# Two engines for the memory banks, a direct split of the sample queries, and a finer first cut of the input

## The chip, the cores and the metric

The kernel runs on one core of a Trainium2 chip. The core has a matrix engine (TensorE, PE in the profile), VectorE (DVE), ScalarE (ACT), GpSimd (POOL) and SyncE (SP), which here only issues transfers. Each engine works through its own list of instructions in a fixed order and waits on semaphores for the others. The metric is the device time of one execution in microseconds; three runs of the kernel before took 2074.03, 2075.16 and 2075.26 us.

## The reference

One layer of a hybrid decoder step: 256 prompt tokens and 8 x 8 sample tokens, 320 rows in all, width 2048, all in fp32. What matters here is the beginning of the layer, the keys and values of the memory, and the queries:

```
def memory_kv(mem, p):
    m = rms_norm(mem, p['norm_mem'])
    k = (m @ p['w_k']).reshape(b_, N_MEM, XA_HEADS, XA_HEAD_DIM)
    v = (m @ p['w_v']).reshape(b_, N_MEM, XA_HEADS, XA_HEAD_DIM)
...
    h = rms_norm(x, p['norm_mix_pre'])
    proj = h @ p['w_in']
...                      # convolution, RWKV-7 mix, w_out, residual
    h = rms_norm(x, p['norm_xa_pre'])
    q = (h @ p['w_q']).reshape(b_, t_, XA_HEADS, XA_HEAD_DIM)
    s = jnp.einsum('bthd,bmhd->bhtm', q, mem_k) * (XA_HEAD_DIM ** -0.5)
...                      # softmax, values, w_o, then a gated ConvFFN
```

The prompt attends to 256 memory tokens whose keys and values are computed here and are outputs too; each of the 8 sample requests has its own keys and values in a cache.

## The kernel before

All products are made of f16 halves: an fp32 number times a power of two is rounded to f16 (the high part, on ScalarE), and what is left over is the low part (on VectorE, one scalar_tensor_tensor). A product then takes three matmuls: high x high, high x low and low x high. `split` (L191 to L193) does this for activations. `wpiece` (L145 to L157) does it for weights: a transfer into `raw` on SP's queue, `whi` on ScalarE (L154), `wlo` on VectorE (L155), in a ring of three buffers each. A piece is 128 x 1024 numbers, so every piece costs VectorE and ScalarE one long operation, and PE uses it right behind.

The start, `rows_in` (L196 to L221): x lies in three tiles of rows (128, 128 and 64), loaded in four groups of 512 columns, three transfers a group. PE turns each 128-column block (L207, through `turn`, L61) into a bank `psn` (five of them), ScalarE writes the high part of h (L213), VectorE the low part (L214). `take(q)` then lets out steps of the first dense product (192 columns of w_in), 8 after each of the first three groups. ScalarE also squares the rows for the norm (L218), with `late` putting a square behind PE's last instruction so far.

The memory projections, `mem_steps` (L940 to L956): w_k has four blocks of 512 columns, w_v four. For each block, two banks `accs[0]` and `accs[1]` (128 memory tokens each) take 3 x 16 matmuls; at the end both are scaled into an SBUF tile (called `memo` in the trace, as it is a part of that tile) and sent off. The program text has both scalings on ScalarE:

```
            for j in range(2):
                kv = kvst[j]
                A.activation(kv, accs[j], AF.Copy, scale=mst[:, j, 7:8])
                SP.dma_start(dst[0, 0, j * P:(j + 1) * P, n, :], kv)
```

The first six blocks (four of w_k, two of w_v; in the text below blocks 0 to 5) run in the pool `psA`, in which these banks are only two, so that a block's first product waits until the block before has left. The last two (blocks 6 and 7) run in `psB`, whose banks are four.

The queries, `q_evac` (L1222 to L1234): for each of 16 feature blocks VectorE scales the bank into `qf` (L1226); the prompt's 256 columns are split into `qp` (ScalarE L192, VectorE L193); then ScalarE scales the 64 sample columns in place (L1228), and GpSimd casts them into `qs` (L1231) and subtracts to get their low part (L1232). `qf` has two buffers. The sample scores `pss` are products with `qs`.

The order: an instruction of ScalarE, VectorE, GpSimd and SP gets its place by a scheduler that simulates times and takes the ready instruction of the highest priority; `tc.high_priority(offset=...)` moves what is inside ahead by so many places (AHEAD is 1200). PE's order in the first part is written by hand, in a planner that lets several generators take turns by a modelled clock. So a change of one engine's operation can move others.

Of the kernel before, what the change touches and what calls it, by code (L numbers as in the profile page):

```python
# [12 lines left out]
AF = mybir.ActivationFunctionType  # L13
ALU = mybir.AluOpType
AX = mybir.AxisListType
PSUM = bass.MemoryType.PSUM

P = 128
# [12 lines left out]
SX = 32.0  # L31
# [4 lines left out]
AHEAD = 1200  # L36
# [10 lines left out]
def hybrid_step_kernel(ctx: ExitStack, tc: tile.TileContext, I, O):  # L47
# [148 lines left out]
    def rows_in(pool, psum, loads, gcol, op, ssq, take):  # L196
        tl = []
        for j, (src, rows) in enumerate(loads):
            tl.append((pool.tile([P, D], F32, name=f"xt{j}"), rows))
        for q in range(4):  # L200
            qc = slice(q * 512, (q + 1) * 512)
            with tc.high_priority(offset=(2 * AHEAD if q == 0 else AHEAD)):
                for (xt, rows), (src, _) in zip(tl, loads):
                    SP.dma_start(xt[:rows, qc], src[:, qc])
            with tc.high_priority(offset=600):
                for f in range(4 * q, 4 * q + 4):
                    ps = psum.tile([P, 512], F32, tag="m", bufs=5, name="psn")  # L207
                    c = 0
                    for xt, rows in tl:
                        turn(ps[:, c:c + rows], xt[:rows, f * P:(f + 1) * P], ident[:rows, :rows])  # L210
                        c += rows
                    oh, ol = op(f)
                    A.activation(oh[:, :c], ps[:, :c], AF.Copy, scale=gcol[:, f:f + 1])  # L213
                    V.scalar_tensor_tensor(ol[:, :c], ps[:, :c], gcol[:, f:f + 1], oh[:, :c], ALU.mult, ALU.subtract)  # L214
            take(q)
            for j, (xt, rows) in enumerate(tl):
                jk = pool.tile([P, 512], F16, tag="njk", bufs=2, name="njk")
                sq = A.activation(jk[:rows], xt[:rows, qc], AF.Square, accum_out=ssq[:rows, j, q:q + 1])  # L218
                if q in (0, 1, 2, 3):
                    late(sq)  # L220

    w_in = I["w_in"][0]
    psA = tc.alloc_tile_pool(name="psA", bufs=3, space=PSUM)
# [10 lines left out]
    with tc.tile_pool(name="p0", bufs=1, side="right", reuse_waits="tile") as p0:  # L234

        def vpt(name="vpt"):
            return psA.tile([P, 512], F32, tag="x", bufs=1, name=name)

        with tc.high_priority(offset=3 * AHEAD):
            ld0 = vr.tile([16, P], F32, tag="ld0", bufs=1, name="ld0")  # L240
            SP.dma_start(ld0, I["norm_mix_pre"][0].rearrange("(t p) -> t p", p=P))
        pt = vpt()
        turn(pt[:, :16], ld0, ident[:16, :16])
        V.tensor_scalar(gx[:, 0:16], pt[:, :16], SX, None, ALU.mult)
        lora_evac = {}
        first_ = dense_steps(psA, w_in, KD, [(5120, 192)], [(0, 0, 96), (0, 96, 96)], opn(h1), T, lambda mi, acc: lora_evac["small"](mi, acc))
        xp, xs_ = I["x_prompt"][0], I["x_sample"].rearrange("b t d -> (b t) d")
        rows_in(p0, psA, [(xp[0:128], 128), (xp[128:256], 128), (xs_, 64)], gx[:, 0:16], opn(h1), xss, lambda q: [next(first_) for _ in range((8, 8, 8, 0)[q])])
        ldm = vr.tile([26, P], F32, name="ldm")
        SP.dma_start(ldm[0:24, :], I["rwkv_mu"][0, 0:3072].rearrange("(t p) -> t p", p=P))  # L250
        SP.dma_start(ldm[24:26, :], I["rwkv_mu"][0, 3264:3520].rearrange("(t p) -> t p", p=P))
        ld3 = vr.tile([2, 96], F32, name="ldL")
        SP.dma_start(ld3, I["rwkv_mu"][0, 3072:3264].rearrange("(t p) -> t p", p=96))
        ld5 = vr.tile([NB, 3520], F32, name="ldS")
        SP.dma_start(ld5, I["state_shift"][0])
        ld2 = vr.tile([80, P], F32, name="ldR")
        for n, nm in enumerate(vR_names):
            SP.dma_start(ld2[8 * n:8 * n + 8, :], I[nm][0].rearrange("(t p) -> t p", p=P))
        ld4 = vr.tile([CW, W], F32, name="ldC")
        SP.dma_start(ld4, I["conv_dw"][0])  # L260
        ld = vr.tile([112, P], F32, name="ldD")
        for n, nm in enumerate(vD_names):
            SP.dma_start(ld[16 * n:16 * n + 16, :], I[nm][0].rearrange("(t p) -> t p", p=P))
        pt = vpt()
        turn(pt[:, :26], ldm, ident[:26, :26])
        turn(pt[:96, 128:130], ld3, ident[:2, :2])
        V.tensor_copy(vecR[:, 80:106], pt[:, :26])
        V.tensor_copy(muL, pt[:96, 128:130])
        pt = vpt()
        for t in range(26):  # L270
            c0 = t * P + (192 if t >= 24 else 0)
            turn(pt[:, NB * t:NB * t + NB], ld5[:, c0:c0 + P], ident[:NB, :NB])
        for z in range(2):
            turn(pt[:96, 256 + NB * z:256 + NB * z + NB], ld5[:, 3072 + 96 * z:3168 + 96 * z], ident[:NB, :NB])
        V.tensor_copy(stR.rearrange("p b t -> p t b"), pt[:, 0:208].rearrange("p (t b) -> p t b", b=NB))
        V.tensor_copy(stL.rearrange("p b t -> p t b"), pt[:96, 256:272].rearrange("p (t b) -> p t b", b=NB))
        pt = vpt()
        turn(pt[:, :80], ld2, ident[:80, :80])
        V.tensor_copy(vecR[:, 0:80], pt[:, :80])
        pt = vpt()  # L280
        for c in range(8):
            turn(pt[:, 32 * c:32 * c + CW], ld4[:, c * P:(c + 1) * P], ident[:CW, :CW])
        V.tensor_copy(cdw, pt[:, 0:256].rearrange("p (c j) -> p c j", j=32)[:, :, 0:CW])
        pt = vpt()
        turn(pt[:, :112], ld, ident[:112, :112])
        V.tensor_copy(vecD, pt[:, :112])
        with tc.high_priority(offset=0):
            xm = p0.tile([P, 3, 2], F32, name="xm")
            V.tensor_reduce(xm[:, :, 0], xss[:, :, 0:4], AX.X, ALU.add)
            V.tensor_scalar(xm[:, :, 0], xm[:, :, 0], 1.0 / D, 1e-6, ALU.mult, ALU.add)  # L290
            G.tensor_tensor(xm[:, :, 1], xm[:, :, 0], nhalf[:, 0:3], ALU.pow)
            V.tensor_scalar(xm[:, :, 1], xm[:, :, 1], 0.5 * INV, None, ALU.mult)
            dg = p0.tile([P, 3, P], F32, name="xdg")
            V.tensor_tensor(dg, ident.unsqueeze(1).broadcast_to([P, 3, P]), xm[:, :, 1:2].broadcast_to([P, 3, P]), ALU.mult)
            pt = vpt()
            for j in range(3):
                mm(pt[:, j * P:j * P + (P if j < 2 else 64)], ones, dg[:, j, 0:P if j < 2 else 64], True, True)
            V.tensor_copy(rh, pt[:, :T])
# [641 lines left out]
    def mem_steps(src, dst, ns, psum):  # L940
        for n in ns:
            accs = [psum.tile([P, 512], F32, tag="acc", name="acck", **({"bufs": 2} if psum is psA else {})) for _ in range(2)]
            for k0 in range(0, KD, 2):
                hi, lo = wpiece(src, k0, 2, [(n * 512, 512)])
                for j in range(2):
                    for k in range(2):
                        kt, c, cols = k0 + k, slice(k * 512, (k + 1) * 512), slice(j * P, (j + 1) * P)
                        mo = memo[kt // 8][:, kt % 8]
                        mm(accs[j], mo[:, 0, cols], hi[:, c], kt == 0, False)
                        mm(accs[j], mo[:, 1, cols], hi[:, c], False, False)  # L950
                        mm(accs[j], mo[:, 0, cols], lo[:, c], False, kt == KD - 1)
                        yield 1.5
            for j in range(2):
                kv = kvst[j]
                A.activation(kv, accs[j], AF.Copy, scale=mst[:, j, 7:8])  # L955
                SP.dma_start(dst[0, 0, j * P:(j + 1) * P, n, :], kv)  # L956


# [263 lines left out]
    def q_evac(f0):  # L1222
        def f_(mi, acc):
            f = f0 + mi
            qf = bw.tile([P, T], F32, tag="qf", name="qf")
            V.tensor_tensor(qf, acc[:, :T], rq, ALU.mult)  # L1226
            split(qp[:, f, 0, :], qp[:, f, 1, :], qf[:, 0:256], SX)
            A.activation(qf[:, 256:320], qf[:, 256:320], AF.Copy, scale=SX)  # L1228
            v_ = qf[:, 256:320].rearrange("p (j b e) -> p j b e", b=2, e=8)
            dh, dl = (qs[f // 4 % 2][:, f % 4, z].rearrange("p j (b e) -> p j b e", e=40)[:, :, :, 0:8] for z in range(2))  # L1230
            G.tensor_copy(dh, v_)  # L1231
            G.tensor_tensor(dl, v_, dh, ALU.subtract)  # L1232
            qdone[0] += 1
        return f_  # L1234

# [429 lines left out]
```

## Time and profile before

| | before |
|---|---|
| median of 3 runs | 2075.16 us (2074.03 to 2075.26) |
| profiled execution | 2076.79 us |
| its span | 2075.1 us |
| PE busy | 2001.3 us, 96% |
| VectorE busy | 1394.6 us, 67% |
| ScalarE busy | 990.9 us, 48% |
| GpSimd busy | 592.1 us, 29% |

The span is the stretch that the profiler sees of one execution; the execution's own time is 1.7 us longer. Busy shares are means over stages that differ. A wait is read from a timeline: an instruction's start, its length, and in brackets how long its engine stood idle before it and what released it. Operations on one engine can overlap a little at their ends, so a start can lie just before the end of the one ahead.

### The profile page before, as it was taken

What the parts mean: (1) busy time and instruction counts of PE and PEld (TensorE: products, weight loads), DVE (VectorE), ACT (ScalarE), POOL (GpSimd) and SP (SyncE); (2) the same over time, 40 slices, a digit from 0 to 9 for tenths busy, and PEclk for the clock granted to TensorE, in tenths of its full rate; (3) what the DMA queues carried; (4) which work ended last, traced back from release to release, by engine and by line L of the source; (5) the groups of instructions that cost most, each with busy time, mean ns of one, the idle gap of its engine ahead of it and who ended that gap; (6) DMA issues with size and microseconds to landing.
All of it is one profiled execution on the core that took longest, in us unless ns stands there. A gap on an engine that the chain in (4) does not pass through costs nothing.

```text
span 2075.1 us, 44953 instructions
## 1 busy us (share of the span) xinstructions
PE 2001.3 (96%) x17941; PEld 1392.5 (67%) x17941; DVE 1394.6 (67%) x2479; ACT 990.9 (48%) x1710; POOL 592.1 (29%) x908
## 2 busy tenths in 40 slices
PE   8989999999999999989999999999999999999998
PEld 6766666666454676556677667777777777777777
DVE  5699787987866636877774696666666666444343
ACT  5444435445545535665663454444444444533331
POOL 3635435444012211300001242444444443000000
PEclk9999999999999999999999999999999999999999
DMA  6543333332547765767765455555555555555552
GB/s 189 149 117 110 88 105 91 107 96 77 174 136 218 235 198 188 242 211 246 251 207 164 131 148 159 162 163 163 163 163 163 163 163 160 162 172 183 163 155 90
DMA packets 301999, 333.34 MB, mean 161 GB/s; under 512 B 33882, under 2 KB 227237, under 8 KB 301764
## 3 DMA queue, kind: packets, MB, share of 16 engines
q1 hardware_dynamic: 301788, 330.46, 53.0%
q8 instruction: 141, 2.31, 0.5%
q14 instruction: 70, 0.57, 0.1%
HBM read 319.90 MB, written 11.22 MB: 160 GB/s over the span
## 4 chain that ended last, share of the span: by engine, by line
PE 79%; DVE 9%; DMA 5%; ACT 2%; issue 2%; POOL 2%; SPq 0%; DVEq 0%; POOLq 0%; ACTq 0%
PE acc L57 62%; PE acck L57 7%; DMA rawkv<-in_cache_mem_v_dram 3%; DVE wlo L155 2%; PE pX L57 1%; DVE cvmix L825 1%; DVE vl L1280 1%; PE pk L61 1%; DMA rawkv<-out_dram 1%; ACT vh L1279 1%; PE psZ L57 1%; PE psX L57 1%; PE pSc L57 1%; PE pU L57 1%; PE pSn L57 0%
## 5 line engine op out<-in xcount | busy, mean ns | idle before, releaser
L57 PE MATMUL acc<-h,whi 128*128 128x320 f16 (+1 forms) x4736 | 984.0, 302 | 11.7 <-DVE h L1163 4.3
L155 DVE SCALAR_TENSOR_TENSOR wlo<-raw,whi 128x1024 f16<-128x1024 f32 (+1 forms) x512 | 626.4, 1226 | 449.6 <-ACT whi L154 446.5
L57 PEld LDWEIGHTS <-whi 128*128 128x128 f16 (+1 forms) x7080 | 686.3, 99 | 279.1 <-issue 13.9
L154 ACT ACTIVATE whi<-raw 128x1024 f16<-128x1024 f32 (+1 forms) x512 | 533.0, 1043 | 596.5 <-PE acc L57 498.8
L57 PE MATMUL acc<-h,wlo 128*128 128x320 f16 (+1 forms) x2368 | 704.1, 302 | 0.0
L57 PEld LDWEIGHTS <-wlo 128*128 128x128 f16 (+1 forms) x3540 | 348.6, 98 | 144.0 <-issue 7.6
L57 PE MATMUL acc<-act,whi 128*128 128x320 f16 x1320 | 269.6, 299 | 0.0
L57 PE MATMUL acc<-act,wlo 128*128 128x320 f16 x660 | 196.6, 299 | 0.0
L57 PE MATMUL acck<-whi,memo 128*128 128x512 f16 x512 | 151.3, 380 | 2.0 <-ACT memo L955 2.0
L825 DVE SCALAR_TENSOR_TENSOR cvmix<-GX,cdw,cvmix 128x320 f32<-128x320 f32 x240 | 144.5, 602 | 1.7
L1510 POOL COPY nF<-U 128x9 f32<-128x9 f32 x88 | 49.3, 560 | 302.0 <-DVE U L1509 299.0
L57 PEld LDWEIGHTS <-memo 128*128 128x128 f16 x768 | 72.7, 98 | 82.4 <-issue 3.5
L1507 POOL COPY U<-stF 128x16 f32<-128x16 f32 x88 | 127.4, 1453 | 0.9 <-ACT stF L1495 0.9
L1145 POOL TENSOR_TENSOR sums<-sums,bsq 128x320 f32<-128x320 f32 x33 | 37.8, 1146 | 241.3 <-ACT bsq L1139 239.7
L57 PE MATMUL acck<-wlo,memo 128*128 128x512 f16 x256 | 95.6, 379 | 0.3 <-DVE wlo L155 0.3
L1515 DVE SCALAR_TENSOR_TENSOR C<-U,fdw,C 128x336 f32<-128x336 f32 x176 | 91.2, 558 | 0.0
L1513 ACT ACTIVATE C<-U,fdw 128x336 f32<-128x336 f32 x88 | 55.8, 659 | 31.3 <-DVE U L1509 30.9
L1508 DVE TENSOR_TENSOR U<-acc,rs 128x256 f32<-128x256 f32 x88 | 36.8, 418 | 39.4 <-PE acc L57 39.4
L1280 DVE SCALAR_TENSOR_TENSOR vl<-rawkv,vh 128x1024 f16<-128x1024 f32 x31 | 37.3, 1224 | 32.4 <-ACT vh L1279 32.2
L1231 POOL CAST qs<-qf 128x64 f16<-128x64 f32 x16 | 10.0, 623 | 161.6 <-ACT qf L1228 161.6
L335 POOL TENSOR_TENSOR pb<-pb,rh 128x256 f32<-128x256 f32 (+1 forms) x28 | 27.4, 980 | 100.3 <-ACT pb L332 86.8
L57 PE MATMUL acc<-oopb,whi 128*128 128x320 f16 x256 | 53.7, 299 | 1.2 <-DVE oopb L193 1.0
(466 smaller groups left out, 2535.7 us busy)
## 6 DMA issues: line engine op xcount, KB each, us to landing
raw<-in_w_up_dram SPq DMA_DIRECT2D x352, 256.0 KB
raw<-in_w_down_dram SPq DMA_DIRECT2D x71, 512.0 KB
raw<-in_w_in_dram SPq DMA_DIRECT2D x52, 512.0 KB
raw<-in_w_in_dram SPq DMA_DIRECT2D x64, 256.0 KB
raw<-in_w_k_dram SPq DMA_DIRECT2D x32, 512.0 KB
raw<-in_w_v_dram SPq DMA_DIRECT2D x32, 512.0 KB
raw<-in_w_out_dram SPq DMA_DIRECT2D x32, 512.0 KB
rawkv<-in_cache_mem_k_dram SPq DMA_DIRECT2D x32, 512.0 KB
```

The costliest lines, as they stand in the source:

```text
L57: pe[0] = TE.matmul(out, lhsT=lhsT, rhs=rhs, start=start, stop=stop, skip_group_check=skip)
L154: A.activation(hi[:, :n], raw[:, :n], AF.Copy, scale=SW)
L155: V.scalar_tensor_tensor(lo[:, :n], raw[:, :n], SW, hi[:, :n], ALU.mult, ALU.subtract)
L335: G.tensor_tensor(pb[:w, 1:257], pb[:w, 1:257], rh[:w, 0:256], ALU.mult)
L825: late(V.scalar_tensor_tensor(o_, i_, cdw[:, c, j:j + 1], o_, ALU.mult, ALU.add))
L1145: (V if f > 11 else G).tensor_tensor(ssum, ssum, sq, ALU.add)
L1280: V.scalar_tensor_tensor(vl, raw, SX, vh, ALU.mult, ALU.subtract)
L1507: G.tensor_copy(us[:, :, 0:2], stF[:, :, :, j])
L1508: V.tensor_tensor(U[:, 2:258], acc[:, 0:256], rf[:, 0:256], ALU.mult)
L1510: G.tensor_copy(nF[:, :, 0, j], U[:, 256:338:10])
L1513: A.activation(c, U[:, 0:336], AF.Identity, bias=fdw[:, 3, j:j + 1], scale=fdw[:, 0, j:j + 1])
L1515: V.scalar_tensor_tensor(c, U[:, t_:t_ + 336], fdw[:, t_, j:j + 1], c, ALU.mult, ALU.add)
```

## The change

Three edits. The first 512 columns of the input are loaded in two groups of 256 columns (six transfers, all at the higher priority), the dense steps are handed out as 2, 6, 8 and 8, and there are 15 squares in place of 12. Of a memory block's two banks the first is scaled on VectorE and the second on ScalarE, both with a priority of 3600 places. The sample part of `qf` is split directly, on ScalarE and VectorE, ahead of the prompt's part; the scaling in place and GpSimd's two operations are gone.

```
@@ -197,13 +197,14 @@
         tl = []
         for j, (src, rows) in enumerate(loads):
             tl.append((pool.tile([P, D], F32, name=f"xt{j}"), rows))
-        for q in range(4):
-            qc = slice(q * 512, (q + 1) * 512)
-            with tc.high_priority(offset=(2 * AHEAD if q == 0 else AHEAD)):
+        cuts = (0, 2, 4, 8, 12, 16)
+        for q, (fa, fb) in enumerate(zip(cuts, cuts[1:])):
+            qc = slice(fa * P, fb * P)
+            with tc.high_priority(offset=(2 * AHEAD if q < 2 else AHEAD)):
                 for (xt, rows), (src, _) in zip(tl, loads):
                     SP.dma_start(xt[:rows, qc], src[:, qc])
             with tc.high_priority(offset=600):
-                for f in range(4 * q, 4 * q + 4):
+                for f in range(fa, fb):
                     ps = psum.tile([P, 512], F32, tag="m", bufs=5, name="psn")
                     c = 0
                     for xt, rows in tl:
@@ -215,9 +216,7 @@
             take(q)
             for j, (xt, rows) in enumerate(tl):
                 jk = pool.tile([P, 512], F16, tag="njk", bufs=2, name="njk")
-                sq = A.activation(jk[:rows], xt[:rows, qc], AF.Square, accum_out=ssq[:rows, j, q:q + 1])
-                if q in (0, 1, 2, 3):
-                    late(sq)
+                late(A.activation(jk[:rows, 0:(fb - fa) * P], xt[:rows, qc], AF.Square, accum_out=ssq[:rows, j, q:q + 1]))
 
     w_in = I["w_in"][0]
     psA = tc.alloc_tile_pool(name="psA", bufs=3, space=PSUM)
@@ -245,7 +244,7 @@
         lora_evac = {}
         first_ = dense_steps(psA, w_in, KD, [(5120, 192)], [(0, 0, 96), (0, 96, 96)], opn(h1), T, lambda mi, acc: lora_evac["small"](mi, acc))
         xp, xs_ = I["x_prompt"][0], I["x_sample"].rearrange("b t d -> (b t) d")
-        rows_in(p0, psA, [(xp[0:128], 128), (xp[128:256], 128), (xs_, 64)], gx[:, 0:16], opn(h1), xss, lambda q: [next(first_) for _ in range((8, 8, 8, 0)[q])])
+        rows_in(p0, psA, [(xp[0:128], 128), (xp[128:256], 128), (xs_, 64)], gx[:, 0:16], opn(h1), xss, lambda q: [next(first_) for _ in range((2, 6, 8, 8, 0)[q])])
         ldm = vr.tile([26, P], F32, name="ldm")
         SP.dma_start(ldm[0:24, :], I["rwkv_mu"][0, 0:3072].rearrange("(t p) -> t p", p=P))
         SP.dma_start(ldm[24:26, :], I["rwkv_mu"][0, 3264:3520].rearrange("(t p) -> t p", p=P))
@@ -286,7 +285,7 @@
         V.tensor_copy(vecD, pt[:, :112])
         with tc.high_priority(offset=0):
             xm = p0.tile([P, 3, 2], F32, name="xm")
-            V.tensor_reduce(xm[:, :, 0], xss[:, :, 0:4], AX.X, ALU.add)
+            V.tensor_reduce(xm[:, :, 0], xss[:, :, 0:5], AX.X, ALU.add)
             V.tensor_scalar(xm[:, :, 0], xm[:, :, 0], 1.0 / D, 1e-6, ALU.mult, ALU.add)
             G.tensor_tensor(xm[:, :, 1], xm[:, :, 0], nhalf[:, 0:3], ALU.pow)
             V.tensor_scalar(xm[:, :, 1], xm[:, :, 1], 0.5 * INV, None, ALU.mult)
@@ -952,7 +951,11 @@
                         yield 1.5
             for j in range(2):
                 kv = kvst[j]
-                A.activation(kv, accs[j], AF.Copy, scale=mst[:, j, 7:8])
+                with tc.high_priority(offset=3 * AHEAD):
+                    if j:
+                        A.activation(kv, accs[j], AF.Copy, scale=mst[:, j, 7:8])
+                    else:
+                        V.tensor_scalar(kv, accs[j], mst[:, j, 7:8], None, ALU.mult)
                 SP.dma_start(dst[0, 0, j * P:(j + 1) * P, n, :], kv)
 
 
@@ -1224,12 +1227,10 @@
             f = f0 + mi
             qf = bw.tile([P, T], F32, tag="qf", name="qf")
             V.tensor_tensor(qf, acc[:, :T], rq, ALU.mult)
-            split(qp[:, f, 0, :], qp[:, f, 1, :], qf[:, 0:256], SX)
-            A.activation(qf[:, 256:320], qf[:, 256:320], AF.Copy, scale=SX)
             v_ = qf[:, 256:320].rearrange("p (j b e) -> p j b e", b=2, e=8)
             dh, dl = (qs[f // 4 % 2][:, f % 4, z].rearrange("p j (b e) -> p j b e", e=40)[:, :, :, 0:8] for z in range(2))
-            G.tensor_copy(dh, v_)
-            G.tensor_tensor(dl, v_, dh, ALU.subtract)
+            split(dh, dl, v_, SX)
+            split(qp[:, f, 0, :], qp[:, f, 1, :], qf[:, 0:256], SX)
             qdone[0] += 1
         return f_
```

Counted over the whole program, VectorE gets 8 scalings of 128x512 and 16 small subtractions of 128x64 more; ScalarE loses 8 evictions, 16 scalings in place and gets 16 small casts and three more squares; GpSimd loses 32 operations; SP gets three more transfers; PE's instructions are the same in number.

The first place is VectorE at the end of block 0. `cvmix` is a step of the convolution, `Tc`, `Gc` and `u` belong to the RWKV mix, `wlo` is a weight's low part, and `memo<-acck` the eviction. Before, it reads:

```order
L825 SCALAR_TENSOR_TENSOR cvmix<-GX,cdw,cvmix 128x320
L155 SCALAR_TENSOR_TENSOR wlo<-raw,whi 128x1024
L403 TENSOR_TENSOR Tc<-psX,Tc 128x8x8
L825 SCALAR_TENSOR_TENSOR cvmix<-GX,cdw,cvmix 128x320
L404 STREAM_TRANSPOSE Gc<-Tc 128x128
L823 TENSOR_SCALAR cvmix<-GX,cdw,vecR 128x320
L683 COPY u<-pU 64x128
L155 SCALAR_TENSOR_TENSOR wlo<-raw,whi 128x1024
```

Now, on the same engine and in the same place:

```order
L824 SCALAR_TENSOR_TENSOR cvmix<-GX,cdw,cvmix 128x320
L155 SCALAR_TENSOR_TENSOR wlo<-raw,whi 128x1024
L402 TENSOR_TENSOR Tc<-psX,Tc 128x8x8
L824 SCALAR_TENSOR_TENSOR cvmix<-GX,cdw,cvmix 128x320
L958 TENSOR_SCALAR memo<-acck,mst 128x512
L403 STREAM_TRANSPOSE Gc<-Tc 128x128
L822 TENSOR_SCALAR cvmix<-GX,cdw,vecR 128x320
L155 SCALAR_TENSOR_TENSOR wlo<-raw,whi 128x1024
L682 COPY u<-pU 64x128
```

The eviction of the first bank stands behind `Tc` and one convolution step, and ahead of `Gc`.

The second place is VectorE around the end of block 4, where `sh` and `shl` are copies of the shifted rows. Before:

```order
L155 SCALAR_TENSOR_TENSOR wlo<-raw,whi 128x1024 x2
L1038 COPY sh<-pSh 72x128
L155 SCALAR_TENSOR_TENSOR wlo<-raw,whi 128x1024 x3
L1038 COPY sh<-pSh 72x128
L155 SCALAR_TENSOR_TENSOR wlo<-raw,whi 128x1024 x3
L1049 COPY shl<-pSh 9x448
```

Now:

```order
L155 SCALAR_TENSOR_TENSOR wlo<-raw,whi 128x1024 x2
L1041 COPY sh<-pSh 72x128
L155 SCALAR_TENSOR_TENSOR wlo<-raw,whi 128x1024 x3
L1041 COPY sh<-pSh 72x128
L155 SCALAR_TENSOR_TENSOR wlo<-raw,whi 128x1024 x2
L958 TENSOR_SCALAR memo<-acck,mst 128x512
L155 SCALAR_TENSOR_TENSOR wlo<-raw,whi 128x1024
L1052 COPY shl<-pSh 9x448
```

The eviction stands between the last two residuals. The end of block 3 has the same form, with the eviction behind eight residuals and ahead of the ninth.

The third place is ScalarE at the end of block 2, where `yo` and `rwmix` are the RWKV mix's output and its high part. Before:

```order
L780 ACTIVATE yo<-pYt,vecR 128x2x64 x2
L781 ACTIVATE yo<-pYt,vecR 128x64
L154 ACTIVATE whi<-raw 128x1024
L955 ACTIVATE memo<-acck,mst 128x512
L192 ACTIVATE rwmix<-yo 128x320
L154 ACTIVATE whi<-raw 128x1024
L955 ACTIVATE memo<-acck,mst 128x512
L154 ACTIVATE whi<-raw 128x1024 x7
```

Now:

```order
L779 ACTIVATE yo<-pYt,vecR 128x2x64 x2
L780 ACTIVATE yo<-pYt,vecR 128x64
L154 ACTIVATE whi<-raw 128x1024
L192 ACTIVATE rwmix<-yo 128x320
L154 ACTIVATE whi<-raw 128x1024
L956 ACTIVATE memo<-acck,mst 128x512
L154 ACTIVATE whi<-raw 128x1024 x8
```

Of the two evictions one is left, the second bank's; it stands behind `rwmix` and a weight cast, as before.

## Rows read from the trace of the kernel before

**Rows 1.** The page: busy time of each engine, and the chain that ended last.

```profile
PE 2001.3 (96%) x17941; PEld 1392.5 (67%) x17941; DVE 1394.6 (67%) x2479; ACT 990.9 (48%) x1710; POOL 592.1 (29%) x908
...
PE 79%; DVE 9%; DMA 5%; ACT 2%; issue 2%; POOL 2%; SPq 0%; DVEq 0%; POOLq 0%; ACTq 0%
```

**Rows 2.** Windows by stage: length, busy time by engine, granted clock, DMA share, GB/s.

```profile
865.00:895.00 30.00, 25.02 (x168) 17.15 (x166) 18.27 (x21) 12.70 (x15) 4.11 (x4) 0.89 0.64 201
895.00:1060.00 165.00, 157.66 (x1527) 112.63 (x1525) 125.38 (x198) 104.80 (x192) 15.98 (x32) 0.99 0.78 254
```

**Rows 3.** PE's waits: tile waited with, releaser, total us, times, longest.

```profile
PE acc L57 <- ACT whi L154: 4.3, 1, 4.3
...
PE psn L61 <- DMA xt<-in_x_prompt_dram: 3.7, 2, 1.9
...
PE acc L57 <- ACT memo L955: 2.6, 2, 1.5
...
PE acck L57 <- ACT memo L955: 2.0, 2, 1.5
...
PE pss L57 <- POOL qs L1231: 1.4, 2, 0.8
```

**Rows 4.** Timeline of the start, SP then PE: start, length, instruction, idle before.

```profile
1.27 0.88 SPq L204 DMA_DIRECT2D xt<-in_x_prompt_dram  x2
...
3.43 0.50 SPq L204 DMA_DIRECT2D xt<-in_x_prompt_dram  x1
...
4.68 2.85 PE L61 MATMUL psn<-ident,xt 128*128 128x128 f32 x12 [1.86 <-DMA xt<-in_x_prompt_dram]
9.33 0.69 PE L61 MATMUL psn<-ident,xt 128*128 128x128 f32 x2 [1.80 <-DMA xt<-in_x_prompt_dram]
```

**Rows 5.** Single operations, by tile and by line: minimum, median, maximum ns.

```profile
L1266 DVE SCALAR_TENSOR_TENSOR kl<-pk,kh x72: 674/680/693, 811.8 to 1057.0; 128x512 f16<-128x512 f32 x72
...
L955 ACT ACTIVATE memo<-acck,mst x16: 666/670/690, 553.0 to 863.1; 128x512 f32<-128x512 f32 x16
...
L1231 POOL CAST qs<-qf x16: 231/538/1220, 896.4 to 1052.3; 128x64 f16<-128x64 f32 x16
...
L1363 DVE TENSOR_TENSOR ats<-pas,ats x8: 211/214/225, 909.6 to 1069.8; 128x64 f16<-128x64 f32 x8
```

**Rows 6.** Timeline at the end of block 0, VectorE, then PE.

```profile
554.58 0.54 DVE L825 SCALAR_TENSOR_TENSOR cvmix<-GX,cdw,cvmix 128x320 f32<-128x320 f32 x1
...
554.62 0.59 PE L57 MATMUL acck<-whi,memo 128*128 128x512 f16 x2
```

**Rows 7.** Timeline at the ends of blocks 2 and 5, ScalarE and PE.

```profile
626.64 1.04 ACT L154 ACTIVATE whi<-raw 128x1024 f16<-128x1024 f32 x1
...
628.30 0.59 PE L57 MATMUL acck<-whi,memo 128*128 128x512 f16 x2 [1.50 <-ACT memo L955]
...
693.86 1.06 ACT L154 ACTIVATE whi<-raw 128x1024 f16<-128x1024 f32 x1
...
695.54 0.43 PE L57 MATMUL acc<-cvmix,whi 128*128 128x320 f16 x2 [1.50 <-ACT memo L955]
```

**Rows 8.** Timeline at the ends of blocks 3 and 4, VectorE and PE.

```profile
646.21 1.23 DVE L155 SCALAR_TENSOR_TENSOR wlo<-raw,whi 128x1024 f16<-128x1024 f32 x1 [1.36 <-ACT whi L154]
...
647.73 0.59 PE L57 MATMUL acck<-whi,memo 128*128 128x512 f16 x2
...
670.23 1.23 DVE L155 SCALAR_TENSOR_TENSOR wlo<-raw,whi 128x1024 f16<-128x1024 f32 x1 [1.39 <-ACT whi L154]
...
670.83 0.38 PE L57 MATMUL acck<-whi,memo 128*128 128x512 f16 x1
```

**Rows 9.** Timeline before the query projection, SP, ScalarE, PE.

```profile
877.68 0.37 SPq L1196 DMA_DIRECT2D rawkv<-in_cache_mem_v_dram  x1
...
884.29 1.06 ACT L1279 ACTIVATE vh<-rawkv 128x1024 f16<-128x1024 f32 x1 [7.89 <-DMA rawkv<-in_cache_mem_v_dram]
...
886.35 0.98 PE L57 MATMUL acc<-h,whi 128*128 128x320 f16 x3 [4.30 <-ACT whi L154]
```

More of the change, by code (lines that the diff above doesn't have):

```diff
@@ L199, in rows_in @@
             tl.append((pool.tile([P, D], F32, name=f"xt{j}"), rows))
-        for q in range(4):
-            qc = slice(q * 512, (q + 1) * 512)
-            with tc.high_priority(offset=(2 * AHEAD if q == 0 else AHEAD)):
+        cuts = (0, 2, 4, 8, 12, 16)
+        for q, (fa, fb) in enumerate(zip(cuts, cuts[1:])):
+            qc = slice(fa * P, fb * P)
+            with tc.high_priority(offset=(2 * AHEAD if q < 2 else AHEAD)):
                 for (xt, rows), (src, _) in zip(tl, loads):
@@ L205, in rows_in @@
             with tc.high_priority(offset=600):
-                for f in range(4 * q, 4 * q + 4):
+                for f in range(fa, fb):
                     ps = psum.tile([P, 512], F32, tag="m", bufs=5, name="psn")
@@ L217, in rows_in @@
                 jk = pool.tile([P, 512], F16, tag="njk", bufs=2, name="njk")
-                sq = A.activation(jk[:rows], xt[:rows, qc], AF.Square, accum_out=ssq[:rows, j, q:q + 1])
-                if q in (0, 1, 2, 3):
-                    late(sq)
+                late(A.activation(jk[:rows, 0:(fb - fa) * P], xt[:rows, qc], AF.Square, accum_out=ssq[:rows, j, q:q + 1]))
     w_in = I["w_in"][0]
@@ L247, in hybrid_step_kernel @@
         xp, xs_ = I["x_prompt"][0], I["x_sample"].rearrange("b t d -> (b t) d")
-        rows_in(p0, psA, [(xp[0:128], 128), (xp[128:256], 128), (xs_, 64)], gx[:, 0:16], opn(h1), xss, lambda q: [next(first_) for _ in range((8, 8, 8, 0)[q])])
+        rows_in(p0, psA, [(xp[0:128], 128), (xp[128:256], 128), (xs_, 64)], gx[:, 0:16], opn(h1), xss, lambda q: [next(first_) for _ in range((2, 6, 8, 8, 0)[q])])
         ldm = vr.tile([26, P], F32, name="ldm")
@@ L288, in hybrid_step_kernel @@
             xm = p0.tile([P, 3, 2], F32, name="xm")
-            V.tensor_reduce(xm[:, :, 0], xss[:, :, 0:4], AX.X, ALU.add)
+            V.tensor_reduce(xm[:, :, 0], xss[:, :, 0:5], AX.X, ALU.add)
             V.tensor_scalar(xm[:, :, 0], xm[:, :, 0], 1.0 / D, 1e-6, ALU.mult, ALU.add)
@@ L954, in mem_steps @@
                 kv = kvst[j]
-                A.activation(kv, accs[j], AF.Copy, scale=mst[:, j, 7:8])
+                with tc.high_priority(offset=3 * AHEAD):
+                    if j:
+                        A.activation(kv, accs[j], AF.Copy, scale=mst[:, j, 7:8])
+                    else:
+                        V.tensor_scalar(kv, accs[j], mst[:, j, 7:8], None, ALU.mult)
                 SP.dma_start(dst[0, 0, j * P:(j + 1) * P, n, :], kv)
@@ L1226, in f_ @@
             V.tensor_tensor(qf, acc[:, :T], rq, ALU.mult)
-            split(qp[:, f, 0, :], qp[:, f, 1, :], qf[:, 0:256], SX)
-            A.activation(qf[:, 256:320], qf[:, 256:320], AF.Copy, scale=SX)
             v_ = qf[:, 256:320].rearrange("p (j b e) -> p j b e", b=2, e=8)
             dh, dl = (qs[f // 4 % 2][:, f % 4, z].rearrange("p j (b e) -> p j b e", e=40)[:, :, :, 0:8] for z in range(2))
-            G.tensor_copy(dh, v_)
-            G.tensor_tensor(dl, v_, dh, ALU.subtract)
+            split(dh, dl, v_, SX)
+            split(qp[:, f, 0, :], qp[:, f, 1, :], qf[:, 0:256], SX)
             qdone[0] += 1
```

## The prediction

> **What bounds the kernel now.** I read the page's busy line and chain first [rows 1], then windows by stage [rows 2], then the list of what TensorE (PE) waited for [rows 3], then timelines around each place that the change touches, and last the durations of single operations. The reader is to see in [rows 1] that PE is busy for 2001.3 of 2075.1 us and that 79% of the chain that ends last is PE's: only about 74 us of PE idle time can be won at all, and work taken off another engine is worth what a PE wait gets shorter by. [rows 3] gives the waits that the change can reach: for the banks of the memory projections 2.6 us (twice, longest 1.5) and 2.0 us (twice, longest 1.5), for the transposed input 3.7 us (twice), for the sample queries 1.4 us (twice). That is 9.7 us, 0.5% of the span, if every one went and nothing came in its place. The rest is a question of queues: on each engine instructions run in the written order, so I ask behind what each moved instruction now stands.
>
> **The start.** Before, two prompt transfers of 512 columns are issued at 1.27 us, 0.44 us each, the next 512 columns begin at 3.43, PE's first twelve transposes run at 4.68, and PE then idles 1.80 us until 9.33, when that second group lands; from there on it is not idle for the rest of the first 40 us [rows 4]. The change issues six transfers in place of three before the first weights, so the second group's first transfer is issued after three more issues: 3 x 0.44 = 1.3 us later. Four f16 pairs of h are ready sooner, but in the new PE order the first products still stand behind four transposes of the next group, which wait for that later transfer. Between its issue at 3.43 and its landing at 9.33 lie 5.9 us, for a 256 KB transfer: it sits behind others and does not land by its issue alone, so I pass on about half of the 1.3 us: **+0.7 us**. Bounds: -1.8, if the whole idle stretch went, and +2.0, if the transfers also ran slower. Three more squares on ScalarE (15 for 12, on the same columns in all) are hidden by PE's dense stretch and stand at 0; without that cover they would cost a part of a microsecond. On this the Trainium skill ("DMA: Bandwidth & Descriptors", Measured) says that small transfers get a small share of the peak, 32% at 64 KB against 78% at 1 MB, and advises large ones; it speaks against this cut. The wait of [rows 4] agrees in direction only, and by the rule the start would end nearer to my upper bound.
>
> **The memory projections' sixteen evictions.** There are eight column blocks of two banks. Today ScalarE empties both, 0.67 us each, and a block's first bank always before its second. The change gives the first bank to VectorE (a scaling from PSUM, 128x512, fp32) and keeps the second on ScalarE. Its price on VectorE isn't in the trace; the nearest row is the split from a 128x512 bank, 680 ns [rows 5], and I take 0.68 us, the same bank in the same type; bounded by 0.54, a convolution step of 128x320 [rows 6], and 1.23, a weight residual of twice the columns [rows 8]. So 8 x 0.68 = 5.4 us move to VectorE, 8 x 0.67 leave ScalarE. What counts is when each bank comes free:
>
> Block 0: VectorE's new order puts the eviction behind the weight residual, one transposed product and a convolution step. That step ran at 554.58 for 0.54 us, the eviction hence from about 555.05 to 555.7. PE wrote the next block's first product into that bank at 554.62 without waiting [rows 6]. New wait: **+1.1 us**. (0 if VectorE gets there sooner; 1.7 if one more step comes before.)
>
> Block 1: by the same reading VectorE lets the eviction in before PE's next product: 0 (0.7, its own length, if one operation more stands in front).
>
> Block 2: the first bank comes free sooner, but it is not what PE waits for. ScalarE reaches the second bank only after the residual mix and a weight cast, 626.64 for 1.04 us; PE waited 1.50 us until 628.30 [rows 7]. In the new ScalarE order the second eviction still stands behind both, so this wait stays: 0. Block 5 is the same case, with a weight cast at 693.86 ahead of it and 1.50 us until 695.54 [rows 7]: 0. These two make 3.0 of the 4.6 us in [rows 3].
>
> Blocks 3 and 4: VectorE's residuals come at PE's pace and the eviction now stands behind one of them. In block 3 that residual starts at 646.21 for 1.23 us, the eviction would end at about 648.1 and PE's product was at 647.73: 0.35, of which a later PE wait takes up a part, **+0.2**. In block 4 the residual starts at 670.23, the eviction ends at 672.1, the product was at 670.83: 1.25 us; the second bank's wait of 0.5 (the shorter of the two in [rows 3]) is then no longer there: **+0.75** [rows 8].
>
> Blocks 6 and 7 lie just before the query projection. PE's other wait for a bank, 1.1 us (2.6 less 1.5 in [rows 3]), would go, and VectorE, busy nearly without a break there, gets 1.4 us more. I count both as absorbed: PE next stops for 4.30 us until 886.35, since the first weight cast of the query projection stands on ScalarE behind the split of a memory-value tile which waited 7.89 us for its transfer, issued at 877.68 [rows 9]. That transfer follows the three weight transfers in SP's order before and after. I take **-0.3** (-1.5 to +1.5): the stall's end may move with the VectorE split that frees the transfer's buffer. The granted clock of 0.89 of that stretch [rows 2] comes with this stall: PE runs at the lower of its two levels after it, and I expect that again.
>
> **The sample queries.** Per feature block, 16 in all, one ScalarE scaling and two GpSimd operations (a cast of 538 ns in the median and up to 1220 [rows 5], and a subtraction) go; one ScalarE cast of the same size and one VectorE operation of 128x64 come, 0.21 us by the nearest row [rows 5]: 16 x 0.21 = 3.4 us more on VectorE, in a stage in which it is busy for 125.4 of 165 us [rows 2]. The chain to the sample scores loses some 0.5 us each time, and the two PE waits on it, **-1.4 us** [rows 3], go. Behind it the prompt's split comes one VectorE operation later, 0.2 us, hidden as long as scores are not waited for at once; the written PE order changes in this stage too, which may give or take 3 us and which I take as 0.
>
> Sum: 0.7 + 1.1 + 0.2 + 0.75 - 0.3 - 1.4 = +1.05 us on the profiled execution's 2076.79, which stands 1.6 above the median of the runs shown, 2075.16: **2076.2 us** for the median after.
>
> **Rivals.**
> (a) *The banks come free in time.* If VectorE reaches blocks 0, 3 and 4 before PE wants them, and ScalarE, with one eviction less per block, reaches the second bank before the cast in front of PE, all 4.6 us of [rows 3] go, the queries' 1.4 too, and 0.9, half of the idle stretch at the start: 2075.2 - 6.9 = 2068.3. For it: two engines share what one did. Against it: both orders keep the second eviction behind the casts that end the waits of [rows 7], and blocks 0 and 4 behind VectorE work. The Trainium skill ("PSUM — Partial Sum Buffer", Specifications) says that ScalarE and VectorE read PSUM side by side at full rate where they use different banks; by that the pair leaves in one eviction's time, as in this rival. No row here shows two such evictions at once.
> (b) *VectorE becomes the bound.* From block 6 to the attention's end the change adds 1.4 + 3.4 = 4.8 us to it. If PE's waits there come to end on VectorE (splits of keys and values, residuals), these add to the evictions' 2.05 and the start's 0.7, less the queries' 1.4: 2075.2 + 6.1 = 2081.3. It decides from the point at which VectorE's idle time in a stage is used up; [rows 2] leaves 40 us idle in 895 to 1060, which speaks against it, but that idle time mostly lies before casts that PE's pace sets.
> (c) *Nothing reaches PE.* All moved work falls into PE's cover and the query projection's stall takes the rest: 2075.2, give or take 2. It ends like my forecast for whoever measures.
>
> **How the numbers follow.** A difference under 0.2%, 4.15 us, is not told from no change. My forecast, +1 with about 3.5 either way from the bounds above, has a chance of 0.45; (c) 0.2; (a), with parts of it, 0.2; (b) 0.15. Of (a) nearly all lies beyond 0.2%, of the forecast and (c) a small tail on each side, of (b) most: faster 0.21, same 0.62, slower 0.17. The range, 2070.0 to 2080.5, leaves out the ends of (a) and (b).
>
> **What would show it.** Right: in PE's list of waits a new line for the VectorE eviction with about 2 to 2.5 us in two or three waits, of which one near 555 and one near 672; ScalarE evictions still with two waits of about 1.5; no wait for sample queries; a wait of about 4 us for the query projection's cast; PE's second stop at the start ending near 10 in place of 9.33. Wrong: a ScalarE eviction no longer waited for; the stall near 886 gone or doubled; more PE idle time between 895 and 1060 than the 7 us of [rows 2], with VectorE as its end.

## The result: slower, by a wait that the forecast did not have

The changed kernel took 2088.09 us (median of four, 2081.52 to 2091.23) where the kernel before took 2075.21; the ratio on record, which is not that of the two medians, is 1.0056, interval 1.0042 to 1.007. The forecast of 2076.2 and its upper end of 2080.5 were both passed. The profile is of the execution that took 2081.52 us, so what it shows is the smaller part of the loss: 4.7 us of span, where the medians lie 12.9 apart.

The page's busy line, which answers to [rows 1]:

```profile
PE 2002.1 (96%) x17941; PEld 1393.2 (67%) x17941; DVE 1400.7 (67%) x2503; ACT 987.0 (47%) x1708; POOL 577.0 (28%) x876
```

The windows by stage that answer to [rows 2], with one stage more behind them:

```profile
865.00:895.00 30.00, 24.27 (x179) 17.16 (x177) 21.06 (x29) 13.41 (x19) 4.26 (x4) 1.00 0.67 217
895.00:1060.00 165.00, 153.82 (x1503) 111.06 (x1501) 123.25 (x209) 101.94 (x191) 0.00 (x0) 0.99 0.76 249
1060.00:1130.00 70.00, 67.70 (x511) 46.78 (x510) 37.04 (x56) 30.97 (x53) 10.18 (x12) 0.95 0.45 137
```

PE does the same work as before but is busy for 3.8 us less in the 165 us of the attention, and neither VectorE nor ScalarE is busy for longer there. Behind it, the granted clock of 0.95 says that PE ran at the lower of its two levels for a while, where before it did not; ahead of it, in 865 to 895 us, it is the other way round, 1.00 now and 0.89 before.

To place the difference I compared the starts of ScalarE's weight casts one by one, since there are 512 of them in the same order. The changed kernel is 1.6 us late at the 17th, level again at the 177th (828.6 us), 1.6 us early at the 193rd, behind the query projection's stall, and 5.7 us late at the 225th, in the output projection; from there to the end it gives back 1.1 us. **The stretch from the 193rd to the 225th takes 200.8 us before and 208.2 after**, and all of the loss lies in it. Its length less PE's busy time is PE's idle time: 8.9 us before, 15.7 after. So 6.8 of the 7.4 us are PE standing idle. The two windows, before and after:

```profile
887.14:1087.95 200.81, 191.93 (x1788) 135.42 (x1787) 148.80 (x238) 122.60 (x229) 18.20 (x38) 0.98 0.72 234
885.52:1093.69 208.17, 192.47 (x1794) 136.35 (x1792) 149.37 (x254) 122.41 (x228) 0.26 (x4) 0.98 0.69 227
```

PE's waits over the whole span, to be held against [rows 3]:

```profile
...
PE psc L57 <- ACT kh L1266: 4.7, 3, 2.7
...
PE pk L61 <- DVE kl L1267: 3.9, 2, 2.1
...
PE psn L61 <- DMA xt<-in_x_prompt_dram: 3.1, 3, 2.1
...
PE acck L57 <- DVE memo L958: 3.1, 3, 1.8
...
PE acc L57 <- DVE qf L1229: 2.0, 1, 2.0
PE acc L57 <- ACT whi L154: 1.9, 1, 1.9
...
PE acc L57 <- ACT memo L956: 1.5, 1, 1.5
...
PE pss L57 <- DVE qs L193: 1.0, 1, 1.0
```

The first two of these are of the attention: `psc` is a score product of the prompt with transposed keys `kh`, `pk` the transposition of the next keys, which waits until VectorE has emptied a bank. Before, both together were 3.1 us, now they are 8.6. PE's waits in 890 to 1090 us of the kernel before:

```profile
PE pk L61 <- DVE kl L1266: 2.9, 5, 0.8
...
PE psc L57 <- ACT kh L1265: 0.2, 1, 0.2
```

The largest of the new ones, on ScalarE and on PE of the changed kernel (start, length, instruction, idle before):

```profile
953.81 1.06 ACT L1280 ACTIVATE vh<-rawkv 128x1024 f16<-128x1024 f32 x1 [3.62 <-DMA rawkv<-in_cache_mem_v_dram]
954.77 1.55 ACT L1266 ACTIVATE kh<-pk 128x512 f16<-128x512 f32 x3
...
955.40 0.38 PE L57 MATMUL psc<-kh,qp 128*128 128x256 f16 x2 [2.66 <-ACT kh L1266]
```

ScalarE idles 3.62 us for the transfer of a value tile, with three key casts queued behind that cast, and PE waits for the first of them. In the kernel before the same two casts stand in the same order:

```profile
952.95 1.06 ACT L1279 ACTIVATE vh<-rawkv 128x1024 f16<-128x1024 f32 x1 [1.58 <-DMA rawkv<-in_cache_mem_v_dram]
953.92 1.55 ACT L1265 ACTIVATE kh<-pk 128x512 f16<-128x512 f32 x3
...
955.46 0.61 PE L57 MATMUL psc<-kh,qp 128*128 128x256 f16 x2
```

There PE reaches that product without a wait, at the same time: it had stood 0.77 and 0.79 us for sample queries just ahead of it, and the products behind them ran more slowly (the granted clock of 942 to 960 us was 0.91, where the changed kernel has 1.00). The changed kernel scaled its first query bank 2.0 us sooner (893.28 for 895.27). It had lost this lead to a stop of the same kind ahead of this one: ScalarE idled 2.83 us for a value tile until 928.32, key casts stood behind that cast, and PE waited 2.13 us for `pk`, until 931.29; the matching transposition ran at 931.51 before. Further stops put it in arrears: 1.73 us at 987.53 for `pk`, 1.48 at 1010.21 for `psc`, each behind a value cast that had waited for its transfer (2.36 and 2.44 us). PE's order between 895 and 1130 us is another one than before. The prediction took that order for written by hand; in this stage the scheduler makes it. Presumably as sample queries are ready sooner in its own simulation, it packs the sample scores closer (for the second head 87 products in a row and then the prompt's first, where there were 79) and puts some key transpositions behind weight products.

### The profile page after: what moved, and what is told of

Same layout as the page of the kernel before. It is cut to its first block, busy times and chain, and to the rows that moved or that the text cites. A ratio compares the mean times of both kernels' runs of the same rounds, so it can differ in the third digit from the quotient of the medians.

```text
span 2079.7 us, 44921 instructions
## 1 busy us (share of the span) xinstructions
PE 2002.1 (96%) x17941; PEld 1393.2 (67%) x17941; DVE 1400.7 (67%) x2503; ACT 987.0 (47%) x1708; POOL 577.0 (28%) x876
## 4 chain that ended last, share of the span: by engine, by line
PE 48%; DVE 2%; issue 1%; DMA 0%; ACT 0%; POOL 0%; DVEq 0%; POOLq 0%
PE acc L57 46%; DVE wlo L155 0%; DVE xr L1164 0%; PE pos L57 0%; DVE h L1166 0%; PE pk L61 0%; DMA rawkv<-in_cache_mem_v_dram 0%; DVE rz L1163 0%; PE pxt L61 0%; PE pmt L61 0%; PE pav L57 0%; DVE kl L1281 0%; PE psc L57 0%; PE prs L57 0%; PE prb L57 0%
## 5 line engine op out<-in xcount | busy, mean ns | idle before, releaser
L1507 POOL MEMSET U<- 128x2 f32 x88 | 8.5, 98 | 222.2 <-DVE kl L1281 191.9
L57 PE MATMUL acc<-cvmix,whi 128*128 128x320 f16 x256 | 52.1, 299 | 1.5 <-ACT memo L956 1.5
```

Source lines behind the costliest of these rows:

```text
L57: pe[0] = TE.matmul(out, lhsT=lhsT, rhs=rhs, start=start, stop=stop, skip_group_check=skip)
```

## The experiments

Each run stood beside runs of the kernel before on the same chip, whose median was 2075.9 to 2076.0 in all three groups. The stage is the stretch between the two weight casts named above, in each run's profiled execution.

| kernel | median us | ratio, interval | stage us |
|---|---|---|---|
| before | 2075.9 | 1 | 200.8 |
| all three edits, again | 2084.23 | 1.0051 (1.0037 to 1.0064) | 208.2 |
| start alone | 2075.88 | 1.0005 (0.9996 to 1.0014) | 201.5 |
| evictions alone | 2076.64 | 1.0003 (0.9994 to 1.0012) | 200.5 |
| queries alone | 2083.00 | 1.0033 (1.0020 to 1.0046) | 210.5 |
| queries, PE's order of before | 2074.67 | 0.9995 (0.9987 to 1.0003) | 200.5 |
| before, PE's order of queries | 2081.41 | 1.0028 (1.0018 to 1.0039) | 211.6 |
| all three, PE's order of before | 2078.44 | 1.0016 (1.0007 to 1.0024) | 200.2 |
| queries, split second | 2084.11 | 1.0042 (1.0026 to 1.0058) | 210.9 |
| before, new order, keys ahead | 2077.68 | 1.0010 (1.0001 to 1.0019) | 204.7 |
| all three, keys ahead | 2077.01 | 1.0003 (0.9994 to 1.0012) | 204.6 |
| queries, order of before, keys ahead | 2076.01 | 0.9997 (0.9988 to 1.0006) | 201.0 |
| start and evictions | 2077.54 | 1.0004 (0.9995 to 1.0013) | 202.8 |

The profiled execution is the slowest of five for the queries alone, the slowest of seven for before in PE's order of queries, and the fastest of twelve for all three in the order of before. Where PE's order is a new one, the rest of the program behind the stage is 0.7 to 2.9 us shorter than before, so that the stage alone shows more than the loss.

**The changed kernel once more**, with no edit.

> The changed kernel once more, to see how far its executions lie apart and where. Theory A (the attention stage lost its order): all executions share the loss of about 4 to 7 us between 895 and 1090 us, and the ones that take longer add stretches at the lower of TensorE's two clock levels behind PE's new idle gaps there, so that the time follows the granted clock: some 10 us for each 0.005 of it. Theory B (the spread is in the transfers): the slower executions have the same granted clock and longer waits for transfers. Expected by A: 2081 to 2092 with granted clocks of 0.984 to 0.989.

It took 2083.56 to 2088.15 us, and the loss was in the same stage. Of the spread the granted clocks say something. The first four executions were 2081.52 at a mean granted clock of 0.989, 2087.16 at 0.988, 2089.01 at 0.987, 2091.23 at 0.984; of the five here, the two of 2088 us had 0.986 and the three near 2084 had 0.987 to 0.989. So the slower ones had more time at the lower level, as theory A has it; where in the span it lay, no profile of a slower one shows. The two profiled executions lie some 2 us apart, and nearly all of that (1.9) had come before the stage.

**One edit at a time.** The parts of the diff alone; for the queries:

```
-            split(qp[:, f, 0, :], qp[:, f, 1, :], qf[:, 0:256], SX)
-            A.activation(qf[:, 256:320], qf[:, 256:320], AF.Copy, scale=SX)
-            G.tensor_copy(dh, v_)
-            G.tensor_tensor(dl, v_, dh, ALU.subtract)
+            split(dh, dl, v_, SX)
+            split(qp[:, f, 0, :], qp[:, f, 1, :], qf[:, 0:256], SX)
```

> Only the finer first cut of the input; evictions and queries as before. In the trace of the changed kernel the weight casts of the first 400 us come 1.6 us later than before. Theory A: 2075.2 + 1.6 = 2076.8, or less if that delay is absorbed before 520 us. Rival C (a delay at the start shifts everything against the transfers and so brings the slow attention too): 2082 or more.

> Only the memory banks on two engines. Theory A: the three waits for the VectorE eviction cost 3.1 us, those for ScalarE's eviction fall by 2.6, the stall before the query projection moves as before: 2075 to 2077. Rival B2 (VectorE's load is what makes the attention slower): 2080 or more, with PE gaps after 895 us that end on VectorE.

> Only the direct split of the sample queries, ahead of the prompt's. Theory A: this edit alone rewrites PE's order between 895 and 1130 us (scores of the samples come ahead in one block, and PE then stands for key tiles), so it alone is slower: 2080 to 2090, with gaps of 1.5 to 2.7 us before pk and psc products near 931, 955, 987 and 1010. Rivals B2 and C: 2073 to 2075, since two PE waits of 1.4 us together go.

The start and the evictions alone can't be told from no change; the queries alone bring the loss, and in their profile PE waits 5.5 us for `psc` and 4.4 for `pk`. Rivals B2 and C fall as main causes.

**PE's order held.** Each PE instruction is put behind the one that stood ahead of it in another kernel, by a dependency without a semaphore; `RUNS` holds the places of PE's instructions 6600 to 9230 there, as 470 to 489 runs, and `pl` the instructions as the program text brings them. Which engine does the queries and in which order PE works are thus set apart, crosswise:

```
+    want = [pl[a + i] for a, n in RUNS for i in range(n)]
+    for x, y in zip(want, want[1:]):
+        tc.add_manual_dep(y.ins, x.ins.name, mybir.DependencyInfo(mybir.DependencyClass.NoSync, mybir.DependencyReason.DATA), reason="order")
```

> The direct split of the queries alone, but PE's instructions 6600 to 9230 (the query projection, the attention and the start of the output projection) held in the order of the kernel before; the transfers then stand in the order of before too. Theory A (the new order of PE makes the loss, not the new operations): 2074 to 2076, perhaps 1 us under before, since the two GpSimd waits of 1.4 us go. Rival B2 (16 more VectorE operations in front of keys, values and residuals make it): 2081 to 2084, as with the edit alone.

> The kernel before, GpSimd's operations and all, with PE's instructions 6600 to 9230 in the order that the queries edit brings. Theory A: 2081 to 2086, the loss without the edit. Rival B2: 2075 to 2077.

> All three edits with PE's order of before in the same stretch. Theory A: 2074 to 2077, as evictions and start alone are worth nothing that can be measured. Rival B2 or a joint effect of the three: 2080 or more.

> The direct split of the queries alone, but written behind the prompt's split, where GpSimd's operations were; the scheduler makes a third order of PE of it, which differs from both in a thousand places or more. Theory A says only that the time follows that order: 2073 to 2086. If the place of the split ahead of the prompt's were the cause (rival D), this is 2074 to 2076 however PE is ordered.

The loss goes with the order: the new operations in the old order take 2074.67, the old operations in the new order 2081.41. SP's transfers follow PE's order in both (they stand exactly as in the kernel that the order is from), so these runs do not part PE's order from SP's, nor from ScalarE's, which goes with it too, the queries' own operations and a few others aside. Writing the split second makes a third order, and it is as slow: rival D falls. All three edits in the old order were 2078.44, 0.16% over before, more than I expected; the stage was as short as before in its profile, but that is of an execution of 2075.63 us, which has no loss to place, and where the rest lies stays open. The new operations in the old order, PE's waits in 890 to 1090 us:

```profile
...
PE pss L58 <- DVE qs L198: 1.4, 2, 0.7
PE pss L58 <- DVE qf L1231: 1.2, 2, 0.8
```

So the two waits for the sample queries do not go with GpSimd: they end on VectorE now, and are as long. And the old operations in the new order, the same stretch, then ScalarE and PE at the largest:

```profile
PE pk L63 <- DVE kl L1271: 4.7, 2, 2.4
PE psc L58 <- ACT kh L1270: 4.6, 3, 2.5
PE pss L58 <- POOL qs L1236: 2.6, 3, 1.3
```

```profile
1012.56 1.06 ACT L1284 ACTIVATE vh<-rawkv 128x1024 f16<-128x1024 f32 x1 [3.49 <-DMA rawkv<-in_cache_mem_v_dram]
1013.52 1.55 ACT L1270 ACTIVATE kh<-pk 128x512 f16<-128x512 f32 x3
...
1014.15 0.38 PE L58 MATMUL psc<-kh,qp 128*128 128x256 f16 x2 [2.46 <-ACT kh L1270]
```

It is the changed kernel's picture, with GpSimd's operations in it: a value cast that waits for its transfer, key casts behind it, PE behind these.

**Keys ahead of values.** With PE's order held, six value casts on ScalarE are put behind the key casts that stood behind them:

```
+    for v, k in ((8, 31), (11, 36), (17, 49), (20, 54), (26, 67), (32, 70)):
+        tc.add_manual_dep(vs[v].ins, ks_[k].ins.name, mybir.DependencyInfo(mybir.DependencyClass.NoSync, mybir.DependencyReason.DATA), reason="keys")
```

> As the run with the operations of before in the new PE order (2081.4), but on ScalarE the key casts stand ahead of the value cast behind which they stood, at six places; PE's order is the same. Theory A2: in the new order PE comes to the transposed keys and the prompt scores sooner, with less other work left in front of them, and then stands because their key cast waits on ScalarE behind a value cast whose transfer has not landed (gaps of 2.4 us at 932 and 989, 1.2 at 956, 2.5 at 1014, 1.0 at 1063). Then those gaps shrink to under 1 us each and the time is 2074 to 2078. Rival A3 (PE is ahead of the transfers as such, and the wait only moves to the products that need the values): 2080 to 2083 with new gaps at pav.

> All three edits in their own PE order, with the key casts ahead of the value casts at the same six places. Theory A2: 2076 to 2080, some 7 us under the changed kernel. Rival A3: 2084 or more, no better than the changed kernel.

> The queries edit in PE's order of before, which took 2074.7, with the key casts ahead as well. In that order PE's waits behind key casts are already small (psc 0.8 us, pk 2.9 us). Theory A2: 2073 to 2075, little to win. If the value casts become late instead: 2076 to 2079.

With PE's and SP's orders as they were, and with VectorE's low parts of the same tiles moving along with the casts, this takes 3.7 us off the old operations in the new order and 7 to 11 off the changed kernel (2084.23 and 2088.09 in its two groups), which is then level with the kernel before. In it, PE's waits in 890 to 1090 us, and ScalarE around 955:

```profile
PE pav L58 <- ACT ah L1328: 2.7, 2, 1.4
PE acc L58 <- DVE qf L1234: 2.1, 1, 2.1
PE pat L63 <- DVE e L1301: 1.9, 1, 1.9
PE pk L63 <- DVE kl L1272: 1.1, 2, 0.5
```

```profile
954.35 1.58 ACT L1271 ACTIVATE kh<-pk 128x512 f16<-128x512 f32 x3 [1.50 <-PE pss L58]
956.23 1.06 ACT L1285 ACTIVATE vh<-rawkv 128x1024 f16<-128x1024 f32 x1 [0.31 <-DMA rawkv<-in_cache_mem_v_dram]
```

The wait for `psc` is gone from the list and `pk` fell from 3.9 to 1.1; a part moved to the attention-times-value products (`pav`, 1.4 to 2.7), as rival A3 had it for all. The stage is 204.6 us, not 200.8. Its window:

```profile
886.84:1091.41 204.57, 194.39 (x1794) 137.63 (x1792) 149.47 (x254) 122.33 (x227) 0.26 (x4) 0.97 0.70 231
```

PE idles 10.2 us in it, where it was 15.7 in the changed kernel and 8.9 before. The other 2.5 us are PE's busy time, which is longer at a granted clock of 0.97 for 0.98; and behind the stage 2.3 us come back, so that 1.4 are left at the end. In the run with the old operations the idle time fell alike, from 17.3 to 12.6. In the old order the same edit wins nothing: its 2076.01 lies just over theory A2's 2073 to 2075 and is not told from 2074.67 (the intervals overlap).

**Start and evictions together.**

> The start and the evictions together without the queries edit. Each alone was 2075.9 and 2076.6; all three in PE's order of before were 2078.4. If the pair has a joint cost: 2077.5 to 2079. If it has none: 2075 to 2077.

2077.54, on the border of the two cases, ratio 1.0004: a joint cost is not shown. What the three have in the old order beyond that stays open.

## Why the prediction was wrong, step by step

**The step that failed** is the last half sentence on the sample queries: "the written PE order changes in this stage too, which may give or take 3 us and which I take as 0". It cost 7.4 us in the stage of the profiled execution, 9.7 with the queries alone and 10.8 with the order alone, of which 6.3, 6.9 and 8.0 were left at the end; by the medians the queries alone are 7.1 us over the kernel before and the order alone 5.5. What stood in its place: in the new order PE came to waits for key casts that stood on ScalarE behind value casts waiting for their transfers, and its waits for `psc` and `pk` rose from 3.1 to 8.6 us. The 3 us had no row behind them. A loose bound was to be had: ScalarE's idle time before value casts in this stage, by the waits on their transfers, is 28.8 us in the trace of before, and any key cast behind one of them can pass such a wait on to PE. I saw that the order moved and priced it as noise.

**The two waits of 1.4 us for the sample queries**, which I took as gone, did not go: 1.0 us is left in the changed kernel, in one wait, and in the old order it is 1.4, on VectorE's part of the split. The price of the operation itself was right, 218 ns where I took 0.21 us.

**The evictions** came out nearly as worked out. PE's waits for VectorE's evictions are 3.1 us in three places: the two that I gave 1.1 and 1.25 us are 1.06 and 1.78, block 3's is 0.26, and the wait of block 5 is as before:

```profile
554.06 0.61 PE L57 MATMUL acck<-whi,memo 128*128 128x512 f16 x2 [1.06 <-DVE memo L958]
...
671.15 0.60 PE L57 MATMUL acck<-whi,memo 128*128 128x512 f16 x2 [1.78 <-DVE memo L958]
...
695.14 0.43 PE L57 MATMUL acc<-cvmix,whi 128*128 128x320 f16 x2 [1.50 <-ACT memo L956]
```

An eviction takes VectorE 744 ns in the median, not 680. Block 2's wait fell from 1.50 to 0.53, which I had not forecast: the residual mix ahead of it, which waits for GpSimd, came 1.5 us sooner on ScalarE (624.73 for 626.26); why, I did not follow. This much of rival (a) came true. The wait of 1.1 us for a bank before the query projection went, but PE waited for VectorE's weight residuals there, 1.05 us at 862.28 and 1.59 at 872.74; the stall behind took both up, as I had counted.

**The start** can be held against the 0.7 us I took only in part. PE's second stop ended 0.4 us later than before, and the first products came at 10.64, for 9.81 before:

```profile
9.74 1.11 PE L61 MATMUL psn<-ident,xt 128*128 128x128 f32 x4 [2.08 <-DMA xt<-in_x_prompt_dram]
10.64 1.27 PE L57 MATMUL acc<-h,whi 128*96 128x320 f16 x4
```

At the 17th weight cast the delay was 1.6 us, but kernels without this edit were 0.3 to 1.3 us late at the same cast in their own executions, and the other runs with it 0.4 to 1.3; so the edit's own cost there is not told from none, and neither is its time alone.

**The query projection's stall** fell from 4.30 to 1.92 us, and a new wait of 2.0 us came 9 us later, for the first query banks. With both, the first query bank was still scaled 2.0 us sooner than before, a little beyond the lower end of my range, and the next stage lost it. PE's lower level, which I expected there again, did not come: the granted clock of 865 to 895 us was 1.00.

**Rival (b)** had the sign but not the mechanism. What I had named as its mark came, more than 7 us of PE idle time between 895 and 1060 (11.2), and the waits for `pk` do end on VectorE's `kl`. But VectorE was busy for 149.4 of the stage's 208.2 us, where it was 148.8 of 200.8 before, and did not bound it: at 929.41, ahead of a `kl` that PE waited for, it had itself idled 3.19 us for the value cast. What bound it was ScalarE's queue: three key casts held behind one value cast, before which ScalarE idled 3.62 us. The Trainium skill ("PSUM — Partial Sum Buffer", Engine vs sequencer instructions) says that the queues of ScalarE, VectorE and GpSimd are strictly first in, first out; the trace agrees, with that number.

## What to carry to other kernels

Where a scheduler makes the order, an edit's price can be that of the order it brings, many times that of its operations: compare the orders, and hold one of them still to see which of the two was paid. On an in-order engine, ask of each instruction that waits for a transfer who stands behind it; a faster step elsewhere may only bring the others sooner to that wait. A wait on one engine's product need not go when another engine makes it.

## What the runs showed that I had not expected

The changed kernel's first four executions lay 9.7 us apart (2081.52 to 2091.23) and the time rose as the mean granted clock fell from 0.989 to 0.984. A wider spread than before is not shown: the next five lay 4.6 us apart, and those of the kernel before 2.6 in the first group but 6.3 to 7.6 in the three later ones, of 21 to 33. The level of the clock differs: 0.987 in the mean of the changed kernel's nine executions, 0.990 over 78 of the kernel before. The profiled executions of both had 0.989, so the part of the loss that they do not show goes with a lower clock; in which stretch stays open. VectorE took 744 ns to scale a bank of 128x512 from PSUM, 11% more than ScalarE's 670.
